# A hybrid mixer on one Trainium2 core: the gate projection z emitted between the differential heads, in two other PSUM banks

## The chip, the cores and the metric

The kernel runs on one core of one Trainium2 chip, with everything in float32. The metric is the device time of one execution in microseconds (us). TensorE (PE in the profile, with its weight loads as PEld), VectorE (DVE), ScalarE (ACT), GpSimd (POOL) and SyncE (SP, which here issues the loads of the weights) each run a queue of instructions in order and wait for one another by semaphores.

## The reference

A sequence of 256 tokens of width 1024 passes two layers. A layer is a half-weighted feed-forward (ffn1), a mixer, and a second feed-forward (ffn2), each behind a normalisation. The mixer splits one projection into three kinds of heads, concatenates their outputs and projects back:

```
q, k, v       -> window_attention   6 heads, ALiBi, a sink in the softmax, windows of 128
dq, dk, dv    -> diff_attention     4 heads: (softmax(s0) - lam * softmax(s1)) @ v
dqkv, db, da  -> gated_delta        6 heads, two directions, chunks of 64
dz            -> gate of the delta heads: out = norm(delta_out) * silu(z)
x = x + concat(window, diff, delta) @ w_out
```

The delta heads need in each chunk the inverse of a unit lower triangular 64x64 matrix, and then a scan over four chunks that carries a 64x64 state per head. z is 384 columns wide and is used only behind the scan.

## The kernel before

A mixer's work is cut into pieces, each a function that emits instructions: `A` and `c` project, `ir` and `io` build the inverses (rows on VectorE and GpSimd, then block products, L799 and L800), `p:i` projects the queries and keys of the attention heads (L428, then a scaling on VectorE, L659 or L662), `d:h` makes the scores and the softmax of differential head h, `h:h` its transposes (L412), copy (L741), output (L759) and output copies (L761), `w:b` and `hw:b` the same for the window heads in pairs (b, b+3), `ie` ends the inverse (L880 to L892), `f` and `g` are its last block products (L905), `sa`, `sb`, `sc` the scan, `z:0` to `z:3` the gate projection (L439, four matmuls each), `ze` its silu as a tanh (L927 on ScalarE, L928 on VectorE), `on` the norm and the gate, `o` the output projection (L1024), added into x on VectorE (L1031) or through ScalarE and GpSimd (L1028, L1029). A string, `ORDER` (L36 to L44), names the pieces in the order in which they are emitted. A scheduler then places the instructions of each engine; the order of emission is its priority, so an instruction that waits may be overtaken.

What orders the work besides:

- PSUM. Its eight banks are three pools: `pm` of two, `pd` of four, `pt` of two. The table `BANK` (L48 to L51) says which pool a tile comes from. A tile waits until the bank's previous tile has been read. A differential head and a window pair take two score tiles `pss` each; z holds two tiles `pz` from `z:0` to `ze`.
- The weight ring. Weights pass through a ring of `NRAW = 8` buffers `wr`. The loads stand in SyncE's queue in the order in which the pieces use them, up to seven ahead. z has four loads of 384 KB, most others are 512 KB. The next layer's weights use the same ring, and each is split there (L253 on ScalarE into `wh`, L254 on VectorE into `wl`).
- The exponentials of a head lie in a tile `sc` of four buffers.

In `ORDER` the z pieces stand behind the last piece of the scan, `sc:3`. The scheduler moved their matmuls to where TensorE was free: twelve of sixteen stand among the window heads, four in the scan.

Of the kernel before, what the change touches and what calls it, by code (L numbers as in the profile page):

```python
# [36 lines left out]
A:0 A:1 A:2 K N A:3 G V c:1:0 c:1:1 clear c:0:0 c:1:2 GS co:1:0 c:0:1 co:1:1 co:1:2 ce:1 GE GT E:1 qn:1 co:0:0 co:0:1  # L37
c:0:2 co:0:2 ce:0 qn:0 E:0 E:3 qc:1:1 c:2:0 c:2:1 E:2 qc:0:0 qc:1:0 X:0:0 qc:0:1 ic X:1:1 X:0:1 X:1:0 i ir:1:2 ir:2:3
ir:3:4 ir:4:5 ir:5:6 p:15 ir:6:7 ir:7:8 ir:8:9 ir:9:10 ir:10:11 ir:11:12 ir:12:13 ir:13:14 c:2:2 ir:14:15 p:14 p:13
co:2:0 p:16 d:0 ir:15:16 d:2 co:2:1 io:0 co:2:2 p:9 d:1 p:12 d:3 w:0 io:1 h:2 h:1 p:10 h:0 io:2 io:3 h:3 p:11 w:1 w:2  # L40
hw:0 io:4 io:5 ie ce:2 dn hw:1 f g:0 hw:2 g:1 sa:0 sb:0 oT:3:4 sc:0 sa:1 sb:1 sc:1 sa:2 sb:2 sc:2 sa:3 sc:3 z:0 z:1
z:2 z:3 ze on:1 o:0:0 on:0 o:0:1 o:0:2 o:0:3 o:0:4 o:0:5 o:0:6 oT:7 oT:5:6 o:0:7 o:1:0 o:1:1 o:1:2 o:1:3 o:1:4 o:1:5
o:1:6 o:1:7
"""  # L44

NRAW = 8

BANK = dict(  # L48
    pj="pm", pv="pd", pz="pm", py="pm", pss="pm", pg="pt", pgr="pd", ptr="pd", pkq="pt", pe="pd", pq="pd", p1="pd",
    p2="pt", pk="pd", px="pt", pS="pt", po="pd", pw="pd", pT="pd", pso="pd", pto="pd",  # L50
)  # L51

# [1183 lines left out]
```

## Time and profile before

| | us |
|---|---|
| median of 3 runs | 1163.51 (1162.44 to 1164.4) |
| profiled execution | 1162.4 |
| its span in the trace | 1160.6 |
| first mixer | about 199 to 386 |
| second mixer | about 772 to 958 |

The mean granted TensorE clock is 0.978 of full. A row of the timeline gives its start and duration in us, the engine, the line, the operation, output and input by the program's names, shapes, a count where neighbours are joined, and in brackets the idle time before it and what ended that. A group of lines gives a count, then busy time and mean ns, then idle time. TensorE writes two records for a float32 matmul of 256 to 408 columns, such as those of pj, pz and py.

### The profile page before, as it was taken

Reading aid. Unit: us, or ns where it says so; the run is one execution under the profiler, and the core shown is the slowest. Engines: PE = TensorE matmul, PEld = TensorE weight load, DVE = VectorE, ACT = ScalarE, POOL = GpSimd, SP = SyncE. Lnnn points to the kernel's source line nnn. Section 1 sums busy time; section 2 is a strip of 40 time slices with the busy share of each in tenths; the row PEclk is TensorE's granted clock in tenths of the full one; section 3 lists DMA queues with packets and bytes.
Section 4 is the critical chain, followed back from the end, with each engine's and each line's share of the span. In section 5 each row is a group of like instructions: output and inputs, shape, how many; then the busy total and the mean of one; then the engine's idle time right before and its main releaser. Section 6 shows DMA issues by size and latency. Waiting matters only on the chain. (4 is left out here: it accounts for less than half of the span.)

```text
span 1160.6 us, 21957 instructions
## 1 busy us (share of the span) xinstructions
PE 1122.9 (97%) x8970; PEld 1025.6 (88%) x8970; DVE 735.1 (63%) x1442; ACT 523.0 (45%) x967; POOL 82.9 (7%) x135
## 2 busy tenths in 40 slices
PE   7999999998899999999999999999989999999996
PEld 7999999776668999999999999988756789999996
DVE  7666654678746566665566666547886476666643
ACT  6545432263572454544444454414437435445431
POOL 0000002101202100000000000011020020000010
PEclk9999999997899999999999999999978999999998
DMA  9655643521114555565555565534210254556521
GB/s 335 213 184 182 206 165 102 163 79 51 54 56 132 189 174 184 184 204 170 173 173 182 182 201 181 160 117 127 78 51 37 75 193 153 184 183 201 182 89 37
DMA packets 49637, 173.64 MB, mean 150 GB/s; under 512 B 5504, under 2 KB 6784, under 8 KB 49536
## 3 DMA queue, kind: packets, MB, share of 16 engines
q1 hardware_dynamic: 49104, 171.64, 45.1%
q8 instruction: 70, 1.15, 0.4%
q10 hardware_dynamic: 432, 0.60, 0.1%
q14 instruction: 31, 0.25, 0.1%
HBM read 171.17 MB, written 1.05 MB: 148 GB/s over the span
## 5 line engine op out<-in xcount | busy, mean ns | idle before, releaser
L254 DVE TENSOR_TENSOR wl<-wr,wh 128x1024 fp32r<-128x1024 f32 x254 | 310.9, 1225 | 181.9 <-ACT wh L253 181.8
L253 ACT ACTIVATE wh<-wr 128x1024 fp32r<-128x1024 f32 x254 | 267.3, 1053 | 256.2 <-issue 146.4
L261 PE MATMUL ps<-xh,wl 128*128 128x256 f32 x1336 | 378.3, 283 | 0.8 <-DVE wl L254 0.8
L259 PE MATMUL ps<-xh,wh 128*128 128x256 f32 x1336 | 379.0, 284 | 0.1
L260 PE MATMUL ps<-xl,wh 128*128 128x256 f32 x1336 | 378.0, 283 | 0.0
L261 PEld LDWEIGHTS ps<-xh,wl 128*128 128x128 f32 x1336 | 256.4, 192 | 1.2 <-DVE wl L254 1.2
L259 PEld LDWEIGHTS ps<-xh,wh 128*128 128x128 f32 x1336 | 256.4, 192 | 1.0 <-issue 0.6
L260 PEld LDWEIGHTS ps<-xl,wh 128*128 128x128 f32 x1336 | 256.4, 192 | 0.0
L259 PE MATMUL ps<-hh,wh 128*128 128x256 f32 x672 | 190.5, 284 | 0.0
L261 PE MATMUL ps<-hh,wl 128*128 128x256 f32 x672 | 188.0, 280 | 0.0
L260 PE MATMUL ps<-hl,wh 128*128 128x256 f32 x672 | 187.5, 279 | 0.0
L428 PE MATMUL pj<-xf,wr 128*128 128x256 f32 x544 | 132.6, 399 | 2.9 <-issue 2.6
L259 PEld LDWEIGHTS ps<-hh,wh 128*128 128x128 f32 x672 | 125.7, 187 | 3.6
L260 PEld LDWEIGHTS ps<-hl,wh 128*128 128x128 f32 x672 | 126.3, 188 | 0.0
L261 PEld LDWEIGHTS ps<-hh,wl 128*128 128x128 f32 x672 | 126.2, 188 | 0.0
L428 PEld LDWEIGHTS pj<-xf,wr 128*128 128x128 f32 x544 | 106.9, 202 | 19.7 <-issue 3.3
L191 POOL TENSOR_TENSOR sqacc<-sqacc,sqt 128x256 f32<-128x256 f32 x41 | 34.6, 843 | 742.0 <-ACT sqt L187 741.9
L282 ACT ACTIVATE hh<-h 128x256 fp32r<-128x256 f32 x88 | 36.1, 415 | 90.3 <-DVE h L280 90.3
L277 DVE TENSOR_TENSOR t<-ps,f_rb 128x256 f32<-128x256 f32 x88 | 36.9, 424 | 37.7 <-PE ps L261 37.4
L1024 PE MATMUL py<-oT,wr 128*128 128x256 f32 x256 | 59.1, 384 | 0.0
L283 DVE TENSOR_TENSOR hl<-h,hh 128x256 fp32r<-128x256 f32 x88 | 36.8, 423 | 30.4 <-ACT hh L282 30.4
L1024 PEld LDWEIGHTS py<-oT,wr 128*128 128x128 f32 x256 | 47.2, 190 | 7.3 <-DVE x L1031 0.3
(321 smaller groups left out, 1135.7 us busy)
## 6 DMA issues: line engine op xcount, KB each, us to landing
wr<-in_ffn SPq DMA_DIRECT2D x258, 512.0 KB, 3.4
wr<-in_mix SPq DMA_DIRECT2D x50, 512.0 KB, 3.4
wr<-in_mix SPq DMA_DIRECT2D x8, 408.0 KB, 3.1
wr<-in_mix SPq DMA_DIRECT2D x8, 384.0 KB, 3.0
x<-in_x SPq DMA_DIRECT2D x4, 256.0 KB, 4.3
ar<-in_ffn SPq DMA_DIRECT2D x8, 128.0 KB, 3.9
cb<-in_constb SPq DMA_DIRECT2D x1, 588.0 KB, 9.8
out_y<-fo SPq DMA_DIRECT2D x2, 256.0 KB, 2.4
```

The lines of the kernel that those rows point to most:

```text
L191: (eng or nc.gpsimd).tensor_tensor(self.sq, self.sq, t, ALU.add)
L253: nc.scalar.activation(h, w, AF.Copy)
L254: nc.vector.tensor_tensor(lo, w, h.bitcast(F32), ALU.subtract)
L259: mm(out, lhsT=ah, rhs=bh, start=start, stop=False)
L260: mm(out, lhsT=ah, rhs=bl, start=False, stop=False)
L261: mm(out, lhsT=al, rhs=bh, start=False, stop=stop)
L277: nc.vector.tensor_tensor(t[:rows], gate, rb[:rows], ALU.mult)
L282: nc.scalar.activation(hh[:n, j, :], h[:n], AF.Copy)
L283: nc.vector.tensor_tensor(hl[:n, j, :], h[:n], hh[:n, j, :].bitcast(F32), ALU.subtract)
L428: mm(ps[:, 0:S], lhsT=w[:, k * P : (k + 1) * P], rhs=xf[:, k, :], start=k == 0, stop=k == KD - 1)
L1024: mm(ps[:, 0:S], lhsT=st["o", q // NBLK][:, c], rhs=oT[:, k, :], start=k == ks[0], stop=k == ks[-1])
```

## The change

Two edits. In `ORDER`, `z:0` moves ahead of `d:0`, `z:1` ahead of `d:2`, `z:2` behind `d:1`, and `z:3` with `ze` behind `d:3`, ahead of `w:0`. In `BANK`, `pz` goes from `pm` to `pt`, and `pss` from `pm` to `pd`, the pool of four, which it then shares with `pT` and `pso` of the heads and others.

```diff
--- before.py
+++ after.py
@@ -37,16 +37,16 @@
 A:0 A:1 A:2 K N A:3 G V c:1:0 c:1:1 clear c:0:0 c:1:2 GS co:1:0 c:0:1 co:1:1 co:1:2 ce:1 GE GT E:1 qn:1 co:0:0 co:0:1
 c:0:2 co:0:2 ce:0 qn:0 E:0 E:3 qc:1:1 c:2:0 c:2:1 E:2 qc:0:0 qc:1:0 X:0:0 qc:0:1 ic X:1:1 X:0:1 X:1:0 i ir:1:2 ir:2:3
 ir:3:4 ir:4:5 ir:5:6 p:15 ir:6:7 ir:7:8 ir:8:9 ir:9:10 ir:10:11 ir:11:12 ir:12:13 ir:13:14 c:2:2 ir:14:15 p:14 p:13
-co:2:0 p:16 d:0 ir:15:16 d:2 co:2:1 io:0 co:2:2 p:9 d:1 p:12 d:3 w:0 io:1 h:2 h:1 p:10 h:0 io:2 io:3 h:3 p:11 w:1 w:2
-hw:0 io:4 io:5 ie ce:2 dn hw:1 f g:0 hw:2 g:1 sa:0 sb:0 oT:3:4 sc:0 sa:1 sb:1 sc:1 sa:2 sb:2 sc:2 sa:3 sc:3 z:0 z:1
-z:2 z:3 ze on:1 o:0:0 on:0 o:0:1 o:0:2 o:0:3 o:0:4 o:0:5 o:0:6 oT:7 oT:5:6 o:0:7 o:1:0 o:1:1 o:1:2 o:1:3 o:1:4 o:1:5
-o:1:6 o:1:7
+co:2:0 p:16 z:0 d:0 ir:15:16 z:1 d:2 co:2:1 io:0 co:2:2 p:9 d:1 z:2 p:12 d:3 z:3 ze w:0 io:1 h:2 h:1 p:10 h:0 io:2
+io:3 h:3 p:11 w:1 w:2 hw:0 io:4 io:5 ie ce:2 dn hw:1 f g:0 hw:2 g:1 sa:0 sb:0 oT:3:4 sc:0 sa:1 sb:1 sc:1 sa:2 sb:2
+sc:2 sa:3 sc:3 on:1 o:0:0 on:0 o:0:1 o:0:2 o:0:3 o:0:4 o:0:5 o:0:6 oT:7 oT:5:6 o:0:7 o:1:0 o:1:1 o:1:2 o:1:3 o:1:4
+o:1:5 o:1:6 o:1:7
 """
 
 NRAW = 8
 
 BANK = dict(
-    pj="pm", pv="pd", pz="pm", py="pm", pss="pm", pg="pt", pgr="pd", ptr="pd", pkq="pt", pe="pd", pq="pd", p1="pd",
+    pj="pm", pv="pd", pz="pt", py="pm", pss="pd", pg="pt", pgr="pd", ptr="pd", pkq="pt", pe="pd", pq="pd", p1="pd",
     p2="pt", pk="pd", px="pt", pS="pt", po="pd", pw="pd", pT="pd", pso="pd", pto="pd",
 )
 
```

The instructions are the same; where they stand changes on all engines. Here is TensorE in the first mixer before, at the differential head d:1 (`pss<-ddb` and `pss<-dqk` are its scores, `pT` the transposes of head 2, `pj` projections):

```order
L428 MATMUL pj<-xf,wr 128x256 x8
L708 LDWEIGHTS sdiag
L708 MATMUL pss<-ddb,sdiag 128x512
L713 MATMUL pss<-dqk 128x256 x2
L412 MATMUL pT<-cst,sc 128x128 x2
L708 LDWEIGHTS sdiag
L708 MATMUL pss<-ddb,sdiag 128x512
L713 MATMUL pss<-dqk 128x256 x2
L412 MATMUL pT<-cst,sc 128x128 x2
L428 MATMUL pj<-xf,wr 128x256 x8
```

Head 2 is transposed between the two score banks of d:1, one after the other. Now TensorE behind the last differential head, where `pss<-wq` are the scores of w:0 (the products of the query p:12), and `pso` the outputs of the heads 2, 1, 0, 3:

```order
L439 MATMUL pz<-wr,xf 128x384 x4
L675 MATMUL pss<-wq 128x256 x4
L412 MATMUL pT<-cst,sc 128x128 x4
L428 MATMUL pj<-xf,wr 128x256 x4
L759 MATMUL pso<-V,PT 128x64 x4
L412 MATMUL pT<-cst,sc 128x128 x4
L428 MATMUL pj<-xf,wr 128x256 x3
L759 MATMUL pso<-V,PT 128x64 x4
L428 MATMUL pj<-xf,wr 128x256
L412 MATMUL pT<-cst,sc 128x128 x4
L428 MATMUL pj<-xf,wr 128x256 x2
L759 MATMUL pso<-V,PT 128x64 x4
```

The transposes of head 2 have moved behind z:3 and the scores of w:0, and the four heads follow one another. The other twelve z matmuls stand between the differential heads' scores ahead of this place. ScalarE around the end of the inverse, from the exponentials of the last differential head, d:3 (L719), before:

```order
L719 ACTIVATE sc,smd<-pss,mxd 128x256 x2
L741 ACTIVATE PT<-pT 128x512
L728 ACTIVATE sc<-sc,c_3247 128x256 x2
L761 ACTIVATE O<-pso,smd 128x64 x2
L694 ACTIVATE sc,sm<-sc,mx 128x256 x2
L695 ACTIVATE es<-mx,row 128x2
L889 ACTIVATE WA<-Vc 32x384
L892 COPY W<-Vc 32x12x32
L699 ACTIVATE sc<-sc,sm 128x256 x2
L694 ACTIVATE sc,sm<-sc,mx 128x256 x2
L695 ACTIVATE es<-mx,row 128x2
L741 ACTIVATE PT<-pT 128x512
```

and now:

```order
L719 ACTIVATE sc,smd<-pss,mxd 128x256 x2
L927 ACTIVATE zt<-pz,rth 128x384
L889 ACTIVATE WA<-Vc 32x384
L927 ACTIVATE zt<-pz,rth 128x384
L892 COPY W<-Vc 32x12x32 x2
L889 ACTIVATE WA<-Vt 32x384 x2
L719 ACTIVATE sc,smd<-pss,mxd 128x256 x2
L741 ACTIVATE PT<-pT 128x512
L889 ACTIVATE WA<-Vc 32x384
L728 ACTIVATE sc<-sc,c_3267 128x256 x2
L761 ACTIVATE O<-pso,smd 128x64 x2
L741 ACTIVATE PT<-pT 128x512
```

The first copy of a head's transposes (L741) now stands behind the first copy of the inverse (L889), and the exponentials of w:0 (L694) have moved further back. On VectorE the rows L686, L689 and L690 of w:0 have moved from ahead of L880 to behind it. In the scan VectorE has this between two steps now (L961 and L962 begin a step, L967 takes `px` from TensorE, L994 `po`):

```order
L961 TENSOR_TENSOR SC<-pk,negc 128x384
L962 TENSOR_TENSOR SC<-SC,vtok 128x384
L1031 TENSOR_TENSOR x<-x,py 128x256
L254 TENSOR_TENSOR wl<-wr,wh 128x1024
L967 TENSOR_TENSOR SC<-px,bel 128x384
L994 TENSOR_TENSOR SC<-po,egc 128x384
```

A split of the next layer's weights (L254) and an addition into x stand inside the step; before, the split stood behind the gated output of a half of the tokens (L1013). On GpSimd, the addition of a differential head (L729) that stood ahead of the inverse's product L799 stands behind it, and an addition into x (L1029) stands ahead of the state update L983. On SyncE the loads of z stand between those of the projections rather than between those and the loads of the output projection.

## The prediction, made before the changed kernel was run

> **What bounds the kernel now.** I read the page's first part, then the stretch of the first mixer by windows (199 to 386 us), its timeline, and the groups of ScalarE there.
>
> ```profile
> PE 1122.9 (97%) x8970; PEld 1025.6 (88%) x8970; DVE 735.1 (63%) x1442; ACT 523.0 (45%) x967; POOL 82.9 (7%) x135
> ```
>
> The windows give for each stretch its length, each engine's busy time and records, then the clock granted to TensorE:
>
> ```profile
> core 0: us, PE busy (x) PEld busy (x) DVE busy (x) ACT busy (x) POOL busy (x), PEclk, DMA share, GB/s
> 275.00:285.00 10.00, 9.85 (x22) 5.80 (x22) 8.27 (x14) 5.64 (x20) 1.27 (x1) 0.50 0.00 1
> 285.00:295.00 10.00, 9.15 (x35) 6.62 (x35) 9.81 (x14) 3.44 (x11) 1.26 (x1) 0.85 0.17 52
> 295.00:305.00 10.00, 7.08 (x34) 4.67 (x33) 6.00 (x10) 2.45 (x8) 4.94 (x2) 1.00 0.16 54
> 305.00:315.00 10.00, 8.91 (x34) 7.33 (x35) 8.10 (x15) 6.73 (x18) 1.27 (x1) 0.66 0.00 0
> 325.00:335.00 10.00, 10.00 (x39) 5.49 (x39) 4.07 (x16) 9.96 (x34) 0.00 (x0) 1.00 0.01 2
> ```
>
> Over the whole span TensorE is busy 97%, but the 97% is mostly the feed-forward layers. In the rows of the mixer the busiest engine changes. From 285 to 295 VectorE is busy 9.81 of 10. From 295 to 305 nobody is: TensorE 7.08, VectorE 6.00, GpSimd 4.94, which is a chain passing from one to the next. From 325 to 335 ScalarE is busy 9.96 and TensorE 10.00, and TensorE executes only 39 records there. The clock column says how TensorE fared: 0.50 from 275 to 285, about 3 us of half clock in the next row (0.85), and about 6.8 us in the row of 0.66. Gate rows z stand in the 325 row, so the change takes TensorE work out of a full row and puts it where TensorE has room. The question is what the path is there.
>
> ```profile
> 298.13 1.27 POOL L729 TENSOR_TENSOR sc<-sc 128x512 f32<-128x512 f32 x1 [7.00 <-ACT sc L728]
> 299.35 3.72 POOL L799 TENSOR_TENSOR pr<-Vi,pp 128x1024 f32<-128x1024 f32 x1
> 303.10 1.22 DVE L800 TENSOR_REDUCE Vi<-pr 128x64 f32<-128x1024 f32 x1 [4.00 <-POOL pr L799]
> 306.74 0.71 DVE L686 SCALAR_TENSOR_TENSOR sc<-wd,pss 128x512 f32<-128x512 bf16 x1
> 307.48 0.69 DVE L689 TENSOR_REDUCE mx<-sc 128x2 f32<-128x512 f32 x1
> 309.27 0.73 DVE L690 TENSOR_SCALAR mx<-mx,nsink 128x2 f32<-128x2 f32 x1
> 310.62 1.24 DVE L880 STREAM_TRANSPOSE Vc<-Vi 128x1024 f32<-128x1024 f32 x1
> ...
> 324.69 0.51 ACT L694 ACTIVATE sc<-sc,mx 128x256 f32<-128x256 f32 x1
> ...
> 336.80 1.61 PE L905 MATMUL p<-WA,XE 32*32 32x32 f32 x96
> ```
>
> The timeline gives three marks. The inverse ends with the transpose L880 at 310.62. The first exponential of window pair 1 (L694) starts at 324.69, 14.07 us later. The first block product of the inverse (L905) starts at 336.80, 12.11 us after that, and the scan follows. L905 stands on TensorE behind all window heads, so the heads' chain over ScalarE sets when it starts, not the inverse. I price the change by these marks, per mixer.
>
> **Step 1, the end of the inverse.** In the new order the window-0 rows leave VectorE's queue ahead of L880: two L686 (0.71 each), one L689 (0.69) and one L690 (0.73), 2.8 us. The two row maxima of the last differential head come in, where one stood before: about 0.7 (priced as L689, the same reduction of 128x512). On GpSimd the addition L729 that ran 298.13 to 299.40 now stands behind the product L799, which it held up: 1.2 us at most. That is -2.8 + 0.7 - 1.2 = -3.3. Against it stands the projection p:12, whose product with the norm (L659) is in VectorE's queue just ahead of L800, and which now comes behind twelve z matmuls. TensorE's idle time from 275 to 305 is 0.15 + 0.85 + 2.92 = 3.9 us. The 16 z matmuls cost:
>
> ```profile
> 329.06 2.24 PEld L439 LDWEIGHTS pz<-wr,xf 128*128 128x128 f32 x8
> ```
>
> ```profile
> 282.85 6.21 PE L428 MATMUL pj<-xf,wr 128*128 128x256 f32 x16
> ...
> 293.09 3.62 PE L428 MATMUL pj<-xf,wr 128*128 128x256 f32 x16
> ```
>
> Each of them is two records, and 8 records take 2.24 us, 0.28 each: 32 records are 9.0 us at full clock. That is 5 us more than the idle time, unless the half clock goes: the same projection takes 6.21 us at 282.85 and 3.62 at 293.09, so 13 us of half clock hold about 5.5 us of lost time. The two nearly cancel. I let the projection come 0.8 us late and take -2.5. Ends: TensorE stays slow and is 2.1 late, -1.2; the clock is full and VectorE also fills the 1.7 us it is idle in the row of 275 to 285 (8.27), -3.3 - 1.3 = -4.6.
>
> The loads of z (four, 384 KB each) are queued some ten loads earlier. With eight slots they are issued seven loads ahead. TensorE waits for no DMA in these rows, and I cost that at nothing. What covers it is the ring; the loads of the projections behind them come no later, since each slot is freed by the same sequence of reads.
>
> **Step 2, from L880 to the exponentials of window pair 1.** This is the term that decides. Before, head 2's transposes stand between the two score banks of d:1 on TensorE, and its copy (L741) and output copies (L761) follow on ScalarE long before the inverse ends. Now these transposes stand behind the scores of w:0, which wait for the product of p:12 on VectorE. So all four heads' copies come after L880, mixed with tanh and the copies of the inverse, and the scores of w:1 stand on TensorE behind the last head's output (L759). ScalarE's groups, 305 to 337 us:
>
> ```profile
> L699 ACT ACTIVATE sc<-sc,sm 128x256 f32<-128x256 f32 x12 | 5.3, 498 | 1.0 <-DVE sm L697 0.9
> L694 ACT ACTIVATE sc<-sc,mx 128x256 f32<-128x256 f32 x10 | 5.0, 498 | 0.8 <-DVE mx L690 0.6
> L741 ACT ACTIVATE PT<-pT 128x512 f32<-128x512 f32 x7 | 4.0, 590 | 0.0
> ...
> L889 ACT ACTIVATE WA<-Vc 32x384 f32<-32x384 f32 x2 | 1.7, 872 | 0.1
> L892 ACT COPY W<-Vc 32x384 f32<-32x384 f32 x2 | 1.7, 850 | 0.0
> L695 ACT ACTIVATE es<-mx,row 128x2 f32<-128x2 f32 x6 | 1.7, 282 | 0.0
> L761 ACT ACTIVATE O<-pso,smd 128x64 f32<-128x64 f32 x6 | 1.5, 307 | 1.5 <-PE pso L759 1.5
> L889 ACT ACTIVATE WA<-Vt 32x384 f32<-32x384 f32 x2 | 1.0, 520 | 0.0
> L892 ACT COPY W<-Vt 32x384 f32<-32x384 f32 x2 | 1.0, 499 | 0.0
> ...
> L728 ACT ACTIVATE sc<-sc,c 128x256 f32<-128x256 f32 x2 | 0.9, 500 | 1.1 <-DVE c L724 1.1
> ```
>
> Columns: count, busy us, mean ns, and idle time before. In the new order ScalarE executes, between L880's result and the last head's L741: four L889 (2 x 0.87 + 2 x 0.52 = 2.8), one L927 (0.6, priced as the L741; the other stands ahead), four L892 (1.7 + 1.0 = 2.7), two L719 (1.0, priced as the L728, of the same shape), four L741 (2.4), two L728 (1.0), six L761 (1.8), four L694 (2.0), two L695 (0.6), two L699 (1.0): 15.9 us of durations. Its instructions overlap: twelve L699 of 498 ns are busy 5.3 us, not 6.0, a factor of 0.89. I take 0.9: 14.3 us.
>
> Behind it comes a chain that nothing covers: output of the last head, scores of w:1, then VectorE.
>
> ```profile
> 306.09 2.07 PE L675 MATMUL pss<-wq 64*128 64x256 f32 x4 [4.01 <-ACT sc L719]
> ...
> 320.26 1.10 PE L759 MATMUL pso<-V,PT 128*128 128x64 f32 x8
> ```
>
> That is 1.1 for the output, 1.1 for the scores (2.07 in the row above at half clock), 1.3 for two L686 and 1.3 for two L689 (two of 0.7 in the rows of step 1, which overlap a little), and 0.3 for an L690 (half of its row there, 0.73 for a tile of two columns) = 5.1 us. The waits inside the head chain are not in the trace of before; the nearest is the 1.5 us that ScalarE waited for L759 in its group above. Ends: nothing (every wait covered by other copies) and 2.5 (1.5 for one head, and half of it for two more). I take 1.5, since the new ScalarE order puts other copies between a head's L741 and its L761, but not each time. With L880 itself (1.24) the stretch is 1.24 + 14.3 + 5.1 + 1.5 = 22.1 us against 14.07: +8.1.
>
> **Step 3, from there to L905.** The window heads 1 and 2 keep their exponentials, normalisations, transposes and output copies. The twelve z matmuls in it lie in TensorE's waits for ScalarE (9.96 of 10). Their leaving is worth nothing while ScalarE is full; one L741 more and one L927 less cancel. 0, ends -0.6 and +0.6.
>
> **Step 4, the scan and the output projection.**
>
> ```profile
> 365.31 11.06 PE L1024 MATMUL py<-oT,wr 128*128 128x256 f32 x50
> ```
>
> ```profile
> 371.62 1.06 ACT L253 ACTIVATE wh<-wr 128x1024 fp32r<-128x1024 f32 x1 [3.97 <-DMA wr<-in_ffn]
> ```
>
> Four z matmuls leave the scan and projection matmuls take their place: of 64, 19 stand behind the scan's last product instead of 25. By 11.06 us for 50 records, two each, six are 2.7 us. But the slots also come free sooner, and splits of the next layer's weights (L253 on ScalarE, L254 on VectorE) now stand between steps of the scan; on GpSimd an addition into x (L1029) now stands ahead of the state update L983, and waits for its ScalarE copy. One L253 in before waited 3.97 us for its DMA; in the scan such a wait would hold the state. I take one hidden and the other at about half, 2.0: -2.7 + 2.0 = -0.7. Ends: -2.7 and +1.3 (the wait in full).
>
> **The sum.** -2.5 + 8.1 + 0 - 0.7 = +4.9 us a mixer. The second mixer runs the same code in the same order, so +9.8. The profiled execution is 1162.4, which gives 1172.2; the median of the runs shown is 1163.5, 1.1 above the profiled one, so I forecast 1173.
>
> **Where a rule of the Trainium skill differs.** The trace gives half clock in two stretches. One begins at about 275, behind this row:
>
> ```profile
> 274.53 0.59 PE L708 MATMUL pss<-ddb,sdiag 128*128 128x512 bf16 x1 [1.50 <-DVE dqk L662]
> ```
>
> The wait ahead of the first is 1.50 us; ahead of the second it is the 4.01 in the row of step 2. So here a wait of 4 us was not needed for the clock to fall. The Trainium skill, "TensorE: Matmul & The Clock Gate", section "HAM oscillation — how this bites in real kernels", says that the clock stays full while no idle gap of TensorE exceeds about 3.4 us. This case's first stretch does not bear it out, the second does. By the rule, z:3 and the interleaved heads would remove the second stretch, and the result would be nearer to the first rival's than to 1173.
>
> **Rivals.** First, the clock stays full because z fills TensorE's gaps. For it: the 3.9 us idle, and z rows that need no late data. Against: the 1.50 us above. Then step 1 is -4.6, the waits of step 2 are zero (+6.6), the rest stays: +1.3 a mixer, 1162.4 + 2.6 + 1.1 = 1166.
>
> Second, the weight splits stall the scan twice: step 4 is -2.7 + 2 x 3.97 = +5.2 in place of -0.7. For it: L253's wait; against: DMA is busy 0.00 to 0.17 of the time in the windows before the scan, so weights can land early. 4.9 + 5.9 = +10.8, which gives 1185; with one of the two in full, +6.9, 1177.
>
> Third, the other side: TensorE was the bound from 325 to 337 (10.00 of 10). Then the 12 z matmuls, 24 x 0.28 = 6.7 us, leave the path in step 3, and step 2 stays. -2.5 + 8.1 - 6.7 - 0.7 = -1.8 a mixer, 1162.4 - 3.6 + 1.1 = 1160. For it: the full row. Against: weight loads are busy 5.49 there and ScalarE 9.96. It decides from the point where step 3 shortens by more than 4.9 us. The Trainium skill, "Perfetto Trace Analysis", warns that matmul busy time is a bad metric, which speaks against this rival too.
>
> Fourth, steps 1 and 2 cancel, since ScalarE's part of the heads is done partly while L880 waits; about 0 a mixer, 1163.5.
>
> **How the numbers follow.** Forecast 0.45 (1169 to 1177 from the ends of step 2's waits and step 1), full clock 0.18, splits 0.09, TensorE-bound 0.18, nothing 0.10. The range leaves out half of the third rival and most of the second: 1160 to 1179. A change of 0.2% (2.3 us) is about what a measurement here can tell. Faster 0.18, same 0.10, slower 0.72.
>
> **What the profile after would show.** Rows of L439 start between 262 and 308, none after 325. L880 starts near 308. The head-2 transposes stand near 308, not 291.18. The first L694 of pair 1 is near 330 (22 us behind L880) and L905 near 342. A row of L254 stands between L962 and L967. If the third rival holds, L694 to L905 shrinks to about 6 us; if the first holds, the clock column reads 0.9 or more from 275 to 315. I am wrong if L905 starts before 336.8, above all if ScalarE does the heads' copies ahead of L880.

## The result and the profile after

The changed kernel takes 1175.24 us (median of 4 runs, 1174.56 to 1179.2) against 1163.87 for the kernel before on the same chip: a ratio of 1.0107 with a 95% interval of 1.0082 to 1.0131. It is slower, by about 11 us; the forecast was 1173. The span of its profiled execution is 1172.7 us against 1160.6, so the trace has 12.1 us to explain, about 6 a mixer.

First the page's line of engines, then the windows of the first mixer. The columns are those of the rows shown before.

```profile
PE 1114.2 (95%) x8970; PEld 1020.0 (87%) x8970; DVE 745.0 (64%) x1442; ACT 522.1 (45%) x967; POOL 81.4 (7%) x135
```

```profile
275.00:285.00 10.00, 6.52 (x27) 4.06 (x26) 9.79 (x12) 1.93 (x8) 0.00 (x0) 0.91 0.29 97
285.00:295.00 10.00, 10.00 (x42) 7.20 (x41) 9.93 (x16) 6.33 (x22) 2.53 (x2) 0.92 0.25 65
295.00:305.00 10.00, 6.46 (x29) 4.00 (x29) 9.90 (x8) 0.91 (x2) 4.99 (x2) 0.93 0.43 147
305.00:315.00 10.00, 7.18 (x30) 5.58 (x27) 7.10 (x14) 8.65 (x19) 0.00 (x0) 0.67 0.00 0
315.00:325.00 10.00, 10.00 (x57) 8.52 (x55) 4.34 (x12) 7.95 (x26) 1.27 (x1) 0.88 0.17 52
325.00:335.00 10.00, 6.21 (x37) 3.77 (x35) 5.34 (x15) 6.42 (x24) 0.00 (x0) 0.80 0.18 55
335.00:345.00 10.00, 7.62 (x26) 3.81 (x26) 4.11 (x19) 5.27 (x15) 0.00 (x0) 0.52 0.00 0
```

TensorE has the same 8970 instructions; its busy share fell from 97% to 95%, and it is the waiting that grew. The half clock of 275 to 285 is mostly gone (0.50 before, 0.91 now), that of 305 to 315 is where it was (0.66, 0.67), and a new one stands at 335 to 345 (0.52). There nobody is full: TensorE 7.62, ScalarE 5.27. ScalarE in the row of 325 to 335 fell from 9.96 to 6.42.

The timeline of the changed kernel at the marks of the forecast:

```profile
297.96 2.85 PE L439 MATMUL pz<-wr,xf 128*128 128x384 f32 x8
304.36 2.17 PE L675 MATMUL pss<-wq 64*128 64x256 f32 x8 [3.54 <-DVE wq L659]
307.15 1.09 PE L412 MATMUL pT<-cst,sc 128*128 128x128 f32 x4 [0.62 <-ACT sc L719]
313.34 1.46 PE L759 MATMUL pso<-V,PT 128*128 128x64 f32 x8 [2.19 <-ACT PT L741]
...
340.40 2.07 PE L1024 MATMUL py<-oT,wr 128*128 128x256 f32 x4 [0.47 <-ACT oT L751]
...
345.15 1.55 PE L905 MATMUL p<-WA,XE 32*32 32x32 f32 x92
```

```profile
306.45 1.23 DVE L880 STREAM_TRANSPOSE Vc<-Vi 128x1024 f32<-128x1024 f32 x1
...
329.32 0.68 DVE L686 SCALAR_TENSOR_TENSOR sc<-wd,pss 128x512 f32<-128x512 bf16 x1
```

```profile
329.32 0.51 ACT L694 ACTIVATE sc<-sc,mx 128x256 f32<-128x256 f32 x1 [3.18 <-DVE mx L690]
```

The last z matmuls stand at 297.96. The scores of w:0 wait 3.54 us for the scaled query (L659), the first head transposes follow at 307.15, and the outputs of the heads begin only at 313.34. So all head outputs, and the copies ahead of them, lie behind L880 (306.45). The exponential of pair 1 waits 3.18 us for its row maximum, at 329.32. It lies 22.87 us behind L880, 14.07 before.

Below, "into the mixer" means a time from the mixer's first projection (the first `pv` row), which starts at 199.07 us before and at 198.88 now for the first mixer. "The full row of L905" is the row of nearly all its 96 records; in the changed kernel four of them run ahead, at 343.45 and 918.90. The marks, worked out from the timelines, first mixer / second mixer:

| mark | before | after |
|---|---|---|
| scores of w:0 on TensorE | 101.62 / 102.39 | 105.48 / 105.78 |
| end of the inverse, L880 | 111.55 / 110.83 | 107.57 / 107.88 |
| first exponential of pair 1 | 125.62 / 125.48 | 130.44 / 130.75 |
| full row of L905 | 137.73 / 137.59 | 146.27 / 145.43 |
| last product of the scan, end | 166.31 / 166.18 | 175.19 / 174.35 |
| next layer's first matmul | 190.63 / 190.30 | 197.03 / 196.18 |

The loss is 6.4 and 5.9 us, together 12.3.

### The profile page after: what moved, and what is told of

It reads as the page before. It is cut to its first block, busy times and chain, and to the rows that moved or that the text cites. A ratio compares the mean times of both kernels' runs of the same rounds, so it can differ in the third digit from the quotient of the medians.

```text
span 1172.7 us, 21968 instructions
## 1 busy us (share of the span) xinstructions
PE 1114.2 (95%) x8970; PEld 1020.0 (87%) x8970; DVE 745.0 (64%) x1442; ACT 522.1 (45%) x967; POOL 81.4 (7%) x135
## 4 chain that ended last, share of the span: by engine, by line
PE 78%; DVE 15%; ACT 5%; issue 1%; POOL 1%; DMA 0%; DVEq 0%; ACTq 0%; POOLq 0%
PE ps L259 20%; PE ps L261 20%; PE ps L260 20%; PE py L1024 4%; PE pj L428 3%; DVE pr L799 2%; DVE pad L550 2%; PE pv L439 1%; DVE Vi L800 1%; DVE wl L254 1%; PE pso L750 1%; PE ps L345 1%; PE pso L759 1%; DVE c L724 1%; PE pq L625 1%
## 5 line engine op out<-in xcount | busy, mean ns | idle before, releaser
L254 DVE TENSOR_TENSOR wl<-wr,wh 128x1024 fp32r<-128x1024 f32 x254 | 310.9, 1225 | 177.5 <-ACT wh L253 177.4
L1024 PE MATMUL py<-oT,wr 128*128 128x256 f32 x256 | 62.3, 394 | 0.9 <-ACT oT L751 0.9
```

Source lines behind the costliest of these rows:

```text
L254: nc.vector.tensor_tensor(lo, w, h.bitcast(F32), ALU.subtract)
L1024: mm(ps[:, 0:S], lhsT=st["o", q // NBLK][:, c], rhs=oT[:, k, :], start=k == ks[0], stop=k == ks[-1])
```

## The experiments

Two theories on the stretch up to pair 1 were tried first (the score banks, or the z matmuls, put the heads late), and two on the stretch from there to L905 (the clock, or the py matmuls ahead of the heads' outputs).

**Score banks back in the pool of two, z moved.**

```diff
 (against the changed kernel)
-... pss="pd" ...
+... pss="pm" ...
```

> The changed kernel with the score banks pss back in the pool of two; z keeps its new place and its two banks. Theory B (the score banks put the heads late): L880 to the first L694 of pair 1 falls from 22.9 us to 14 to 17, and the time to 1165 to 1170, the part of z that stays. Theory Z (the z matmuls ahead of the window scores put them late): it stays at 21 to 23 us, and the time at 1173 to 1177.

Measured: 1191.47 us (1186.63 to 1198.72), ratio to before 1.024 (1.0196 to 1.0284). L880 comes at 104.87 us into the first mixer and the exponential at 136.86, 32 us behind it. Neither theory came true: to take the bank edit back makes the change worse by 16 us, not better.

**Only the score banks moved.**

```diff
 (against the kernel before)
-... pss="pm" ...
+... pss="pd" ...
```

> The kernel before with only the score banks moved to the pool of four; z stays where it was, behind the scan in the order and among the window heads on TensorE. Theory B: L880 to L694 is 20 to 23 us as in the changed kernel, L694 to L905 stays near 12.1 since z still fills TensorE there, and the time is 1170 to 1174. Theory Z: 14 us and 1162 to 1166.

Measured: 1153.53 us, ratio 0.9906 (0.9892 to 0.9921). It is faster than before by 10.7 us, below both expectations. On TensorE its order around the heads is that of the changed kernel (four transposes behind the scores of w:0, then the heads one after the other), and here are their times:

```profile
283.08 3.72 PE L428 MATMUL pj<-xf,wr 128*128 128x256 f32 x16
...
292.92 2.20 PE L675 MATMUL pss<-wq 64*128 64x256 f32 x8 [4.63 <-DVE c L724]
...
296.91 0.70 PE L412 MATMUL pT<-cst,sc 128*128 128x128 f32 x4
...
299.20 1.10 PE L759 MATMUL pso<-V,PT 128*128 128x64 f32 x8
```

```profile
313.17 1.24 DVE L880 STREAM_TRANSPOSE Vc<-Vi 128x1024 f32<-128x1024 f32 x1
```

```profile
275.00:285.00 10.00, 7.52 (x39) 5.29 (x40) 9.90 (x18) 5.41 (x20) 1.27 (x1) 1.00 0.17 53
```

```profile
321.17 0.51 ACT L694 ACTIVATE sc<-sc,mx 128x256 f32<-128x256 f32 x1
```

The projection p:12 (first row) starts 83.8 us into the mixer, against 94.1 in the changed kernel (its row is quoted below) and 94.0 before, where the row of 275 to 285 had half clock and now has 1.00. The scores of w:0 start at 93.7 instead of 105.5, and the first head output at 100.0 instead of 114.5. L880 comes later than in either kernel (113.9 us into the mixer), because the rows of w:0 on VectorE are ahead of it, but the exponential of pair 1 follows 8.0 us behind it. That the transposes stand behind the scores of w:0 in the order is no loss by itself. What makes them late is the rest of the change, the move of z with its own two banks; the last experiment tells these apart. Which wait the four banks removed was not tested.

**py out of the heads and the scan.**

```diff
 (against the changed kernel)
-... py="pm" ...
+... py="pt" ...
```

> The changed kernel with the output projection's tile py in the pool of z and the scan, so that none of its matmuls can stand among the window heads or in the scan. L694 of pair 1 to the full row of L905 took 15.8 us in the changed kernel (12.1 before). Theory P (the two py matmuls ahead of the heads' outputs cost it): 12 to 13.5 us. Theory C (TensorE has too little work there, its clock falls to half): 14.5 to 16 us, with a granted clock near 0.5 there. The time rises in any case, to about 1185 to 1195, since 21 projection matmuls a mixer move behind the scan (21 x 0.44 us).

Measured: 1188.15 us (one run). With no py matmul ahead of L905, L694 to the full row of L905 is 15.3 us in both mixers (130.51 to 145.78, 129.83 to 145.11), 15.8 and 14.7 in the changed kernel. Here is a window in it:

```profile
335.00:345.00 10.00, 6.07 (x24) 2.75 (x24) 2.34 (x11) 7.49 (x22) 0.00 (x0) 0.50 0.00 0
```

The clock is at half, and the stretch is as long as before the edit to within 0.6 us. The py matmuls were not the cause.

**Idle matmuls where z had been.**

```diff
 (against the changed kernel: a piece of z's shape, in the pool that z left)
+st["pf"] = [self.psum([P, 512], "pf", "pm") for p in range(2)]
+mm(st["pf"][p][:, 0:NB], lhsT=xf[:, k, p * P : (p + 1) * P], rhs=xflat[:, 0:NB], ...)
-... sc:2 sa:3 sc:3 on:1 ...
+... sc:2 sa:3 sc:3 fl:0 fl:1 fl:2 fl:3 on:1 ...
```

> The changed kernel with 16 idle matmuls of z's shape added a mixer, which read nothing new and whose result is not used, where z stood before (13 among the heads, 3 in the scan). Theory C: the clock there is full again, L694 to L905 is 12 to 13 us, and in spite of 16 more matmuls the time falls by 2 to 6 us, to 1169 to 1173. Theory P gives the same mark, since py stands later, but no change of the clock. If neither holds, the added matmuls cost 9 us of TensorE time a mixer and the time rises above 1177.

Measured: 1171.57 us, ratio to before 1.0064 (1.0047 to 1.0081), so 3.7 us less than the changed kernel, whose ratio was 1.0082 to 1.0131, for 32 more matmuls in all. L694 to L905 is 12.31 and 12.30 us. Its windows:

```profile
325.00:335.00 10.00, 9.34 (x52) 6.05 (x52) 5.76 (x16) 6.02 (x21) 0.00 (x0) 1.00 0.17 55
335.00:345.00 10.00, 9.94 (x136) 6.05 (x135) 4.12 (x19) 7.26 (x21) 0.00 (x0) 1.00 0.01 2
```

The granted clock is 1.00 where it was 0.80 and 0.52. Since py too stands later here, the run alone would not decide between the two theories; with the run before, in which py left and little changed, it does. Matmuls in z's old place, useful or not, keep TensorE's clock up among the window heads, and with them the stretch is 3.5 and 2.4 us shorter than in the changed kernel. That the clock alone makes this difference is not shown, as the next run will tell.

**z a sixth as wide.**

```diff
 (against the changed kernel)
+m = 64 if kind == "z" else n
-mm(st[name][p][:, 0:n], ..., rhs=w[:, c], ...)
+mm(st[name][p][:, 0:m], ..., rhs=w[:, c], ...)
```

> The changed kernel with z cut to 64 of its 384 columns (the gate of the first head is used for all six), so that its 16 matmuls stand in the same places and take a fraction of their 9 us. Theory M (TensorE time of z ahead of the projection p:12 makes p:12, the scores of w:0 and then all head outputs late): the scores of w:0 start 97 to 101 us into the mixer (105.5 in the changed kernel, 93.7 with only the banks moved), the first exponential of pair 1 at 123 to 127 (130.4), and the time is 1158 to 1166. Theory O (the new order and the banks cost it, however long z is): 104 to 106, 129 to 131, and 1172 to 1177.

Measured: 1151.31 us, ratio 0.99 (0.9885 to 0.9915), 24 us below the changed kernel with the same instructions, save that z is narrower, in nearly the same order. It is further than theory M had it. The scores of w:0 start 94.39 us into the mixer (105.48), the exponential at 119.89 (130.44).

```profile
286.93 3.67 PE L428 MATMUL pj<-xf,wr 128*128 128x256 f32 x16
...
292.02 1.10 PE L440 MATMUL pz<-wr,xf 128*128 128x64 f32 x8
293.87 2.02 PE L676 MATMUL pss<-wq 64*128 64x256 f32 x8 [0.74 <-DVE wq L660]
...
297.91 1.09 PE L412 MATMUL pT<-cst,sc 128*128 128x128 f32 x4 [0.86 <-issue]
```

Eight z records take 1.10 us there and 2.85 in the changed kernel. Twelve matmuls stand ahead of p:12, 24 records: 3 x (2.85 - 1.10) = 5.3 us less, and p:12 starts 6.6 us sooner into the mixer (87.5) than in the changed kernel (94.1), whose row is this:

```profile
292.93 3.62 PE L428 MATMUL pj<-xf,wr 128*128 128x256 f32 x16
```

The scaled query then comes at 93.83, 11.1 us sooner, since VectorE takes it ahead of the last inverse products instead of behind them. So it is z's time on TensorE ahead of the heads, and one place in VectorE's order that hangs on it.

This run also says something of the stretch behind pair 1. No z stands among its window heads either, and its mean clock from L694 to the full row of L905 is as low as in the changed kernel (0.61 and 0.60 in the two mixers, against 0.57 and 0.65). Yet the stretch takes 12.97 and 12.70 us, not 15.8 and 14.7. So a low clock there need not cost 3.7 us. ScalarE comes into the stretch without a wait in this run, and is idle for 2.4 us of it in the first mixer; in the changed kernel it comes in behind a wait of 3.18 us, and is then idle for 4.9. The clock and the lateness of the heads were not varied apart.

**z behind the scores of w:0, in one piece.**

```diff
 (against the changed kernel)
-p:16 z:0 d:0 ir:15:16 z:1 d:2 ... d:1 z:2 p:12 d:3 z:3 ze w:0
+p:16 d:0 ir:15:16 d:2 ... d:1 p:12 d:3 w:0 z:0 z:1 z:2 z:3 ze
```

> The changed kernel with all four z pieces behind d:3 and the scores of w:0, so that none stands ahead of p:12; TensorE then has 16 z matmuls in one piece between the scores of w:0 and the first head's transposes. Theory M1 (what costs is that p:12 comes late): the scores of w:0 start 93 to 95 us into the mixer, the first exponential of pair 1 at 121 to 125, the time is 1157 to 1164. Theory M2 (any 9 us of TensorE ahead of the head outputs costs the same): the scores are early too, but the exponential is at 128 to 131 and the time 1168 to 1175.

Measured: 1177.99 us, ratio 1.013 (1.0114 to 1.0145).

```profile
293.53 1.24 PE L675 MATMUL pss<-wq 64*128 64x256 f32 x8 [1.76 <-DVE c L724]
294.70 10.59 PE L439 MATMUL pz<-wr,xf 128*128 128x384 f32 x32
305.12 0.60 PE L412 MATMUL pT<-cst,sc 128*128 128x128 f32 x4
305.56 1.89 PE L428 MATMUL pj<-xf,wr 128*128 128x256 f32 x8
314.46 1.76 PE L759 MATMUL pso<-V,PT 128*128 128x64 f32 x7 [7.01 <-ACT PT L741]
```

The scores of w:0 are early (94.09), as M1 has it, and the exponential of pair 1 is late (131.67), as M2 has it. The transposes stand 8 us later than with the banks alone, and then the output waits 7.01 us for their copy, which stands on ScalarE behind the inverse's copies. So p:12 is one way to be late and not the only one: in both places tried at full width ahead of the head outputs, they slide behind the end of the inverse and into ScalarE's copies of it.

**z among the window heads, both bank edits.** Two places were tried, behind the scores of w:2 and behind the first window pair's outputs.

```diff
 (against the changed kernel)
-p:16 z:0 d:0 ir:15:16 z:1 d:2 ... d:1 z:2 p:12 d:3 z:3 ze w:0
+p:16 d:0 ir:15:16 d:2 ... d:1 p:12 d:3 w:0
-... p:11 w:1 w:2 ...
+... p:11 w:1 w:2 z:0 z:1 z:2 z:3 ze ...
 (the second place: hw:0 z:0 z:1 z:2 z:3 ze io:4)
```

> Both bank edits of the changed kernel, with the z pieces and ze behind the scores of w:2, so that 15 of 16 matmuls stand in one piece among the window heads, none in the scan. If z costs nothing where TensorE waits for ScalarE, 1150 to 1155, as with only the score banks moved (1153.5); if the single piece of 15 (8.5 us) holds up the transposes of the window heads, 1156 to 1162.

> As the run with z behind w:2, but the z pieces stand behind the first window pair's outputs, and lie in pieces of 5, 7 and 3 between transposes and outputs; projection matmuls take the place of the four z matmuls in the scan. If z as a filler is free there and the scan filled with projections shortens the tail, 1149 to 1153, below the run with only the score banks moved (1153.5); if the tail gains nothing, 1153 to 1156.

Measured: 1151.31 us, ratio 0.9899 (0.9885 to 0.9914), and 1156.49 us, 0.9943 (0.992 to 0.9965), with runs from 1153.32 to 1158.77. The first is the fastest version with the whole of z, 12 us faster than before. It isn't told apart from the run with only the score banks moved (0.9892 to 0.9921). Both bank edits are in it, so the two banks of z are not what made the changed kernel slow: the place of z is. The second was expected to be the better one and was not. Its mixers differ: the exponential of pair 1 to L905 took 16.3 us in the first and 14.65 in the second.

## Why the prediction was right, and where its steps were not

The forecast of 1173 was 2 us off, and its sign and size held. Most of its signs came true too: the rows of z start between 262.77 and 297.96, the head transposes at 307.15, the exponential of pair 1 at 329.32, and L905 with its first records at 343.45 (342 forecast). The steps, in us a mixer, worked out from the marks of the table:

| step | forecast | first mixer | second |
|---|---|---|---|
| 1, the end of the inverse | -2.5 | -4.0 | -3.0 |
| 2, L880 to pair 1 | +8.1 | +8.8 | +8.2 |
| 3, pair 1 to L905 | 0 | +3.7 | +2.6 |
| 4, L905 to the next layer | -0.7 | -2.1 | -2.0 |
| sum | +4.9 | +6.4 | +5.9 |

That the sum came so near is in part luck: in the first mixer the steps are off by -1.5, +0.7, +3.7 and -1.4 us, and these cancel down to +1.5.

Step 1 held in kind. The rows of w:0 left VectorE ahead of L880, and the product on GpSimd no longer waits behind a head's addition: it begins at 97.1 us into the mixer, 100.3 before. On TensorE the projection p:12 is not late, as the forecast nearly had it: it starts 94.05 us into the mixer, 94.02 before. With the score banks alone it starts at 83.8, so what that edit gains ahead of it, the half clock included, and the time of z cancel. (The price of z was low: 9.0 us from the row of weight loads, 10.59 for all 32 records in the run with z in one piece.) What the forecast missed is what follows on VectorE. The scaled query of p:12 before, and VectorE now:

```profile
298.11 0.40 DVE L659 SCALAR_TENSOR_TENSOR wq<-pj,m_rb 128x256 f32<-128x256 f32 x1
```

```profile
295.94 3.78 DVE L724 SCALAR_TENSOR_TENSOR c<-smd,nlam,c 128x2 f32<-128x2 f32 x1
...
299.83 1.20 DVE L800 TENSOR_REDUCE Vi<-pr 128x64 f32<-128x1024 f32 x1
301.07 2.81 DVE L799 TENSOR_TENSOR pr<-Vi,pp 128x1024 f32<-128x1024 f32 x1
303.80 0.41 DVE L659 SCALAR_TENSOR_TENSOR wq<-pj,m_rb 128x256 f32<-128x256 f32 x1
```

p:12 ends at about the same time in both (296.7 before, 296.6 now), but its scaled query comes 5.9 us later into the mixer (104.92 against 99.04), and 11.8 later than with the banks alone (93.13). VectorE now runs the inverse's L800 and L799 ahead of it, which stood behind it before, and L724, which takes about 0.2 us in its other places in this mixer, spans the whole of the product on GpSimd (295.98, 3.72 us). The inverse did not pay for that: the heads did.

Step 2 held in its number, and its mechanism was the right one: all heads' copies come after L880, mixed with those of the inverse, and the scores of pair 1 wait for the last of them.

```profile
323.83 0.58 ACT L741 ACTIVATE PT<-pT 128x512 f32<-128x512 f32 x1
```

From the end of L880 to the end of this last copy 16.7 us pass (forecast 14.3 + 1.5), and 4.9 from there to the exponential of pair 1 (forecast 5.1). Its reason was incomplete. The forecast laid it to the place of the transposes behind w:0, which is the same with only the score banks moved, and that kernel is faster than before. It treated the two edits as one. They have opposite signs: the edit of the score banks gains 10.7 us alone, and the rest costs 21.7 on top of it (1175.2 against 1153.5).

Step 3 is the step that failed. It priced the leaving of z at nothing while ScalarE is full. ScalarE did not stay full: in the first mixer it has the same work in the stretch (10.95 us, 10.85 before), now in 15.83 us instead of 12.11. TensorE without z fell to half clock (a mean of 0.57, 1.00 before), and ScalarE waited for its outputs L750 (1.52 and 3.42 us). The run with idle matmuls shows that filling TensorE undoes it: the stretch is back at 12.3 us with the clock at 1.00. How much of it is the clock and how much the heads being late stays open, since the run with a narrow z has the same low clock and loses only 0.9 and 0.6 us against before.

Step 4 was mis-sized the other way, and its count was off. The 25 and 19 projections that it took to stand behind the scan's last product are those ahead of the last transposes alone. Here is the row behind these before, and the whole tail now:

```profile
376.86 12.92 PE L1024 MATMUL py<-oT,wr 128*128 128x256 f32 x58
```

```profile
374.00 8.47 PE L1024 MATMUL py<-oT,wr 128*128 128x256 f32 x38
383.76 0.84 PE L412 MATMUL pto<-cst,O 128*128 128x128 f32 x6 [1.28 <-DVE O L1013]
384.44 11.57 PE L1024 MATMUL py<-oT,wr 128*128 128x256 f32 x52
```

At two records each, 54 projections stood there before and 45 now. Nine fewer are 4.0 us by the forecast's own price of 11.06 us for 50 records, and a new wait of 1.28 us for the gated output (L1013) takes part of it back: 21.8 us pass instead of 24.3. The splits of the weights do stand inside the scan (L254 at 364.25, between L962 and L967), but the scan from its first product to its last grew by 0.4 us only, not by 2.0.

Of the rivals, a full clock came true for one stretch of two and was lost again in another. TensorE as the bound of 325 to 337 is refuted: with z gone the stretch grew. The splits stalled little. The rule of the Trainium skill, "TensorE: Matmul & The Clock Gate", section "HAM oscillation — how this bites in real kernels", that TensorE should have no idle gap over about 3.4 us, fits one place and not another: ahead of the stretch of 305 to 315 the trace has a wait of 3.54 us, which exceeds it; ahead of and inside the half clock of 335 to 345 it has waits of 3.25 and 2.46 us, neither of which does.

```profile
332.30 1.11 PE L750 MATMUL pso<-PT,V 128*64 128x256 f32 x2 [3.25 <-ACT PT L741]
...
336.91 1.12 PE L412 MATMUL pT<-cst,sc 128*128 128x128 f32 x4 [2.46 <-ACT sc L694]
```

What stays open besides: a scheduler rebuilds the order of every engine for each of these kernels, so the time that z takes and the order that follows from it were not fully separated. The run with a narrow z comes nearest, with almost the same order on TensorE.

## What to carry to other kernels

A gap on an engine is not slack if what stands behind the gap feeds a chain. Here the z matmuls put ahead of a projection made it start 10 us later into the mixer than it does with the score banks alone; the scores of a window head came late with it, and with these all head outputs. Low-priority work that can go anywhere is better placed where the engine waits for a chain that is already late: behind the scores of w:2 it cost nothing that could be measured, and among the window heads it kept the clock up. And when a change has two edits, price each alone: here one gained 10.7 us and hid in the loss of the other.

## What the runs showed of the hardware

Work of no use made the kernel faster: 16 idle matmuls a mixer took 3.7 us off, and the clock that was granted to TensorE among the window heads rose with them from 0.80 and 0.52 to 1.00.

A VectorE instruction on 128x2, L724, took 3.78 and 3.80 us in the two mixers of the changed kernel where it ran beside a product on GpSimd of 3.72 and 3.75 us, and about 0.2 us in its other six places in that kernel. What held it was not tested.
